# Two row tiles of the output projection inside the last group of the attention loop; the last group's sums by one product and its quotients from PSUM

## The chip, the cores and the metric

The kernel runs on one core of one Trainium2 chip. The core has a matrix engine (TensorE, PE in the profile), a vector engine (VectorE, DVE), an activation engine (ScalarE, ACT), a general engine (GpSimd, POOL) and an engine that here only issues transfers (SyncE, SP). Each works through its own instructions in order; semaphores hold an instruction back until what it needs is done. Products are written to PSUM, eight banks of 128 x 512 numbers in f32, and read from there by DVE or ACT; everything else lies in SBUF. The metric is the time of one execution on the device in microseconds (us), as the median over runs.

## The reference, cut to what matters

A two-layer encoder over 1024 tokens of width 1024. Layer 0 mixes tokens by grouped-query attention (16 query heads of width 64, 4 key/value heads), layer 1 by pooling; each layer then has a cross-attention into 256 memory tokens and a gated MLP. All of it is f32. The change lies at the end of the attention of layer 0 and at the begin of its output projection:

```python
def axial_gqa_attention(h, w_qkv, q_gain, k_gain, w_o):
    ...
        scores = jnp.einsum('bkgqd,bksd->bkgqs', q_blk, kt).astype(jnp.float32)
        p = jax.nn.softmax(scores, axis=-1).astype(vt.dtype)
        return jnp.einsum('bkgqs,bksd->bkgqd', p, vt)
    ...
    o = o.transpose(1, 0, 4, 2, 3, 5).reshape(b, s, N_HEADS * HEAD_DIM)
    return o @ w_o

x = x + axial_gqa_attention(rmsnorm(x, attn_norm[ia]), attn_w_qkv[ia],
                            attn_q_gain[ia], attn_k_gain[ia], attn_w_o[ia])
x = x + memory_cross_attention(rmsnorm(x, xattn_norm[i]), ...)
```

## The kernel before, in words

**Split products.** Every operand of an accurate product is kept as a high and a low half (`high` on ACT, `low` on DVE: the high half is the rounded number, the low half what is left). `mm3` (L758) makes one product of three matmuls: high by high (L761), high by low (L762), low by high (L763). A block of 128 rows by 512 columns of a projection over width 1024 is eight such triples, 24 matmuls, into one PSUM bank.

**The attention loop.** `attention` works through 16 groups, `G = 0..15`: a group is one half of the 1024 queries (512) and one pair of heads; groups 0 to 7 are the first half, 8 to 15 the second. A group has four steps `d = 0..3`, each with two key tiles. Per step PE makes the scores of two key tiles (`plan_scores`, L1225, into the tiles `pT`), ACT the exponentials (L1232) into a tile `X` (an `E` in the code), PE the products with the values (`plan_values`, L1267, into `pO`) one step later, and besides the scores of coming groups once more for their row maxima (`plan_peaks`, L799, into `pS`, read by DVE at L805). There are none of these left to make in the last group.

**The sums of a group.** The softmax denominators are column sums of the exponentials. DVE adds the two tiles of a step (L1276) into a scratch tile `acc[G, d]`; POOL adds these onto `acc[G, 0]` (`more`, L1279); `plan_sum` then multiplies by ones (L1303: PE, 4 matmuls for one `acc`) into a bank `pS`. In the last group, POOL adds only `acc[G, 1]`, and the product runs over three tiles, `d = 0, 2, 3`: 12 matmuls. After that comes a chain over several engines: ACT copies the sums to SBUF (L1307), a transfer brings the distinct ones to 8 x 128 (L1312), DVE takes reciprocals (L1316), two transfers (L1321, L1326) spread them out over 128 x 512 through DRAM, POOL multiplies the output by them (L1330), and ACT and POOL write high and low halves of it (L674, L1338) into the tiles `OT`, the left operand of the output projection. `OT[0]` and `OT[1]` belong to the first half of the queries, `OT[2]` and `OT[3]` to the second.

**PSUM.** In the loop there are two `pT` of two banks, three `pS` and one `pO`; a `pS` is taken by a pair of peaks (two of them) or by one sum. After the loop a pool of four `pB` of one bank and two `pA` of two lies over the same eight banks; a tile of it waits for the last reader of what was there.

**What sets the order.** The order on every engine in the loop comes from a planner (class `Plan`): `plan.add(kind, size, emit, reads, writes, take, uses, late=...)` enters an operation with a cost of its kind; PE keeps the order in which operations are entered, the others are placed by when their inputs are due to be ready and by a due time, worked back from those who read them or given by `late`. `take` names pool buffers (`("A", b)`: one of the three `pS`). Transfers are planned on SP in the same manner.

**The output projection.** Its weights come in two column halves. The first, `self.ws`, is loaded and split in group 14 (`plan_rows`: four pieces, transfer L1361, `high` and `low` at L674 and L677). The second is loaded by `load_rows` after the loop (transfer L696 into a scratch tile `scr`, L682 on ACT, L683 on DVE, four pieces). There are six scratch tiles; `acc`, `ON` (a group's output and its reciprocals) and the pieces of weights all live in them. The blocks `(n, t)`, column half `n` and row tile `t`, are made by `rows_by`: `gemm` (24 matmuls into a `pB`) and `add` (L1761, DVE adds it to `X[t]`), in the order that `Seven.begin` gives:

```python
        steps = ((0, 0), (0, 2), (1, 0), (1, 2), (0, 4), (1, 4), (0, 6), (1, 6),
                 (0, 1), (1, 1), (0, 3), (1, 3), (0, 5), (0, 7), (1, 5), (1, 7))
        turns = {3: 0, 4: 2, 6: 4, 8: 6, 10: 1, 12: 3, 15: 5}
```

After each block comes `save` (SP, L321: that half of `X[t]` to DRAM), after a second half the row's norm (ACT L742, POOL L734 and L736, DVE L325, in place on `X[t]`), and at the steps named in `turns` PE transposes a normed row tile (L330). Row tiles 0 to 3 need only `OT` of the first half of the queries; `(0, 4)` is the first that needs groups 8 to 15.

**The residual.** `plan_x` loads row tiles 0, 2, 4, 6 of `x` (L1415) into tiles that held exponentials and have come free.

Of the kernel before, what the change touches and what calls it, by code (L numbers as in the profile page):

```python
# [635 lines left out]
class Kernel:  # L636
# [140 lines left out]
    def attention(self):  # L777
# [416 lines left out]
        with tc.tile_pool(name="at", bufs=1, reuse_waits="tile") as at, self.psum("psl", 0, 0) as self.ps:  # L1194
# [63 lines left out]
            def plan_values(G, d):  # L1258
# [34 lines left out]
            def plan_sum(G):  # L1293
                half, m = GROUPS[G]
                b, own, used = ("sum", G), ("on", G, 1), [("on", G)]
                ds = (0,) if G < last else (0, 2, 3)

                def emit():
                    T[b] = self.ps.tile([P, 512], F32, name="pS", bufs=3)
                    for d in ds:  # L1300
                        u = acc.pop((G, d))
                        for x in range(2):
                            nc.tensor.matmul(T[b][x * HD:(x + 1) * HD], ones, u[:, x * 512:(x + 1) * 512],  # L1303
                                             start=d == ds[0], stop=d == ds[-1])
# [23 lines left out]

                def scale():
                    nc.gpsimd.tensor_tensor(out=ON[G][:, :512], in0=ON[G][:, :512], in1=ON[G][:, 512:], op=OP.mult)  # L1330

                def part(j, lo):
# [4 lines left out]
                    if lo:  # L1337
                        nc.gpsimd.tensor_tensor(out=l, in0=src, in1=h.bitcast(F32), op=OP.subtract)  # L1338
                    else:
                        self.high(h, src)  # L1340
                plan.add("product", 4.0 * len(ds), emit, [("acc", G, d) for d in ds], [b], [("A", b)], [("acc", G, d) for d in ds])
                plan.add("copy", 512, copy, [b, ("on", G)], [own], uses=[b, *used])
                plan.add("load", 0.2, spread, [own], [("rs", G)], uses=used)
                plan.add("recip", 128, inverse, [("rs", G)], [("rs", G)])
                plan.add("load", 0.2, park, [("rs", G)], [("inv", G)])
                plan.add("load", 0.5, back, [("inv", G)], [own], uses=used)
                plan.add("pool", 512, scale, [own, ("on", G)], [("on", G)], uses=used)
                for j in range(2):
                    k = ("OT", G, j)
                    plan.add("copy", 256, partial(part, j, 0), [("on", G)], [k], [("half", None)] * 8 if (m, j) == (0, 0) else (), used,  # L1350
                             late=14.0)
                    plan.add("pool", 256, partial(part, j, 1), [("on", G), k], [k], uses=used, late=15.0)
# [24 lines left out]

            self.ws = []
            with tc.manual_schedule():
# [5 lines left out]
                def peak():  # L1385
                    for it in [next(ahead, None)]:
                        if it:
                            plan_peaks(*it)
                for n, (G, d) in enumerate(steps):
# [359 lines left out]
    def rows_by(self, lhs, X, free, rhs, free_w):  # L1749
# [4 lines left out]
        def gemm(n, t):  # L1754
            ps[t] = self.psB()
# [3 lines left out]
        def add(n, t):  # L1759
            x = X[t][:, n * 512:(n + 1) * 512]  # L1760
# [581 lines left out]
    def run(self):  # L2342
# [14 lines left out]
        steps = self.rows_by(lhs, X, free, lambda n, k: self.blk(ws[n], k, slice(0, 512)), lambda n: R.put(*ws[n]))  # L2357
# [48 lines left out]
```

## Time and profile before

| what | value |
|---|---|
| median of 3 runs | 2414.16 us (2412.76 to 2416.49) |
| profiled execution, its own time | 2419.23 us |
| its span, first to last instruction | 2417.4 us |
| granted TensorE clock, mean | 0.997 |
| DVE busy | 78% of the span |
| ACT busy | 49% |
| POOL busy | 18% |
| the 240 reads of peaks (L805) | 152.9 us of DVE |
| the pair adds of the loop (L1276), 49 | 80.6 us of DVE |

The page of the profile gives each engine's busy time, a strip of 40 slices over the span, the chain of work that ended last, and the costliest groups of instructions. Beside it the trace answers views: the instructions of an engine in order of time (start, duration, engine, line, operation, tile written <- tiles read, count; in brackets the idle time before it and what ended that), groups by line, and busy time by stretch. A matmul's duration overlaps with that of the next; what one costs is the distance from start to start.

### The profile page before, as it was taken

What the parts mean: (1) busy time and instruction counts of PE and PEld (TensorE: products, weight loads), DVE (VectorE), ACT (ScalarE), POOL (GpSimd) and SP (SyncE); (2) the same over time, 40 slices, a digit from 0 to 9 for tenths busy, and PEclk for the clock granted to TensorE, in tenths of its full rate; (3) what the DMA queues carried; (4) which work ended last, traced back from release to release, by engine and by line L of the source; (5) the groups of instructions that cost most, each with busy time, mean ns of one, the idle gap of its engine ahead of it and who ended that gap; (6) DMA issues with size and microseconds to landing.
All of it is one profiled execution on the core that took longest, in us unless ns stands there. A gap on an engine that the chain in (4) does not pass through costs nothing.

```text
span 2417.4 us, 33999 instructions
## 1 busy us (share of the span) xinstructions
PE 2392.6 (99%) x12484; PEld 1939.3 (80%) x12484; DVE 1887.3 (78%) x2689; ACT 1182.0 (49%) x1894; POOL 426.1 (18%) x465
## 2 busy tenths in 40 slices
PE   8999999999999999999999999999999999999998
PEld 8984544688998888888888888798888888887887
DVE  6789999549873798888887767987389888888875
ACT  6335556425562555455454427555255554545442
POOL 6757777410010000000000003011000000000001
PEclk9999999999999999999999999999999999999999
DMA  7000001425951234333387533696123332338852
GB/s 254 19 2 10 19 15 45 139 89 191 322 199 44 88 98 129 109 88 109 103 288 243 190 100 124 205 324 216 51 86 113 105 109 87 114 119 272 261 187 101
DMA packets 323004, 324.41 MB, mean 134 GB/s; under 512 B 32533, under 2 KB 253053, under 8 KB 322837
## 3 DMA queue, kind: packets, MB, share of 16 engines
q1 hardware_dynamic: 322837, 322.23, 41.5%
q8 instruction: 99, 1.62, 0.3%
q14 instruction: 68, 0.56, 0.1%
HBM read 234.58 MB, written 82.64 MB: 131 GB/s over the span
## 4 chain that ended last, share of the span: by engine, by line
PE 90%; DVE 3%; issue 3%; DMA 2%; POOL 1%; ACT 1%; SPq 0%; POOLq 0%; DVEq 0%; ACTq 0%
PE pB L761 23%; PE pB L763 23%; PE pB L762 22%; PE pO L1267 4%; PE pT L1225 3%; PE pA L763 3%; PE pA L761 3%; PE pA L762 3%; PE pS L799 2%; DVE R L677 1%; PE pB L330 1%; PE pS L1303 1%; PE pA L2282 0%; DMA scr<-X 0%; DMA scr<-in_ffn_w_down 0%
## 5 line engine op out<-in xcount | busy, mean ns | idle before, releaser
L761 PE MATMUL pB<-R,R 128*128 128x512 f32 (+1 forms) x2764 | 1026.0, 371 | 3.7 <-DVE scr L446 1.2
L763 PE MATMUL pB<-R,R 128*128 128x512 f32 (+1 forms) x2760 | 1018.3, 369 | 1.4 <-DVE R L677 1.2
L762 PE MATMUL pB<-R,R 128*128 128x512 f32 (+1 forms) x2764 | 1019.3, 369 | 0.2 <-DVE R L677 0.2
L761 PEld LDWEIGHTS pB<-R,R 128*128 128x128 f32 x2764 | 522.6, 189 | 95.4 <-DVE scr L446 2.5
L763 PEld LDWEIGHTS pB<-R,R 128*128 128x128 f32 x2760 | 521.8, 189 | 89.5 <-DVE R L677 3.2
L762 PEld LDWEIGHTS pB<-R,R 128*128 128x128 f32 x2764 | 522.8, 189 | 86.3 <-DVE R L677 1.2
L674 ACT ACTIVATE R<-scr 128x512 fp32r<-128x512 f32 (+3 forms) x372 | 268.7, 750 | 230.6 <-DMA scr<-Gs 59.3
L734 POOL TENSOR_SCALAR ms<-ss 128x1 f32<-128x1 f32 (+2 forms) x93 | 26.0, 280 | 1655.6 <-ACT R L742 1284.1
L677 DVE TENSOR_TENSOR R<-X,R 128x512 fp32r<-128x512 f32 x374 | 253.1, 689 | 67.8 <-ACT R L674 67.2
L677 DVE TENSOR_TENSOR R<-scr,R 128x512 fp32r<-128x512 f32 (+2 forms) x332 | 283.8, 884 | 25.7 <-ACT R L674 25.1
L674 ACT ACTIVATE R<-X 128x512 fp32r<-128x512 f32 x374 | 231.9, 630 | 133.4 <-PE pB L762 64.0
L444 ACT COPY scr<-pB 128x512 f32<-128x512 f32 x156 | 91.1, 584 | 180.1 <-PE pB L763 172.9
L805 DVE TENSOR_REDUCE nm<-pS 128x1 f32<-128x512 f32 x240 | 152.9, 684 | 18.2 <-PE pS L799 16.4
L1970 DVE TENSOR_TENSOR X<-pB,X 128x512 f32<-128x512 f32 (+1 forms) x145 | 99.4, 687 | 82.3 <-PE pB L763 81.2
L1232 ACT ACTIVATE X<-pT 128x1024 f32<-128x1024 f32 x128 | 125.2, 1023 | 76.6 <-PE pT L1225 73.0
L761 PE MATMUL pA<-R,R 128*128 128x512 f32 (+1 forms) x420 | 150.6, 358 | 0.0
L763 PE MATMUL pA<-R,R 128*128 128x512 f32 (+1 forms) x420 | 150.2, 358 | 0.0
L762 PE MATMUL pA<-R,R 128*128 128x512 f32 (+1 forms) x420 | 150.0, 357 | 0.0
L1267 PE MATMUL pO<-X,X 128*64 128x512 f32 x512 | 123.8, 605 | 0.0
L446 DVE TENSOR_TENSOR scr<-pB,scr 128x512 f32<-128x512 f32 x156 | 107.2, 687 | 11.5 <-PE pB L763 11.4
L1225 PE MATMUL pT<-R,R 64*128 64x512 f32 x768 | 104.7, 393 | 1.3 <-ACT X L1232 1.3
L1815 DVE SCALAR_TENSOR_TENSOR scr<-scr,conv 128x1023 f32<-128x1023 f32 x66 | 84.7, 1284 | 20.9 <-ACT scr L1810 18.9
(179 smaller groups left out, 2882.3 us busy)
## 6 DMA issues: line engine op xcount, KB each, us to landing
X<-in_ffn_w_up SPq DMA_DIRECT2D x82, 512.0 KB
Gs<-X SPq DMA_DIRECT2D x105, 256.0 KB
scr<-in_ffn_w_down SPq DMA_DIRECT2D x45, 512.0 KB
scr<-Gs SPq DMA_DIRECT2D x35, 512.0 KB
scr<-in_xattn_w_kv SPq DMA_DIRECT2D x32, 512.0 KB
scr<-Gs SPq DMA_DIRECT2D x42, 384.0 KB
Wt<-scr SPq DMA_DIRECT2D x44, 256.0 KB
Gs<-scr SPq DMA_DIRECT2D x42, 256.0 KB
```

The source lines that it names most:

```text
L444: self.nc.scalar.copy(out, p)
L446: self.nc.vector.tensor_tensor(out=out, in0=p, in1=out, op=OP.add)
L674: self.nc.scalar.activation(hi, src, AF.Copy)
L677: self.nc.vector.tensor_tensor(out=lo, in0=src, in1=hi.bitcast(F32), op=OP.subtract)
L761: mm(out, ah, bh, start=start, stop=False)
L762: mm(out, ah, bl, start=False, stop=False)
L763: mm(out, al, bh, start=False, stop=stop)
L805: nc.vector.tensor_reduce(NM[G][:, 2 * n + x.start:2 * n + x.stop], S, axis=AX.X, op=OP.max, negate=True)
L1225: nc.tensor.matmul(T[G, kt % 2][:, x * 512:(x + 1) * 512], left, right, start=first and (i, j) == (0, 0), stop=shifted or (not first and i ...
L1232: nc.scalar.activation(E[G, kt], T[G, kt % 2], AF.Exp)
L1267: nc.tensor.matmul(O[G][x * HD:(x + 1) * HD], V32[kt // 4][:, kt % 4, m // 4 * 2 + x], E[G, kt][:, x * 512:(x + 1) * 512], start=kt == 0, ...
L1970: nc.vector.tensor_tensor(out=x, in0=banks[b][:, c], in1=x, op=OP.add)
```

## The change

1. **Blocks (0, 0) and (0, 2) move into the loop.** A new `plan_out(t, ks)` enters products of a block for the `k` in `ks`, into a tile `pS`; `plan_added(t)` enters the add. In the last group, where a place for peaks finds none left, one triple of block (0, 0) is entered: eight places, eight triples. Block (0, 2) is entered whole, between the last products with the values and the last sum. The two adds are entered after the last sum; nothing in the plan reads what they write. `rows_by` skips both blocks' `gemm` and `add`; the saves stay.
2. **The last group's sums by one product.** `acc[15, 2]` and `acc[15, 3]` are added onto `acc[15, 0]` by DVE (`acc[15, 1]` still by POOL), and 4 matmuls replace 12.
3. **The last group's quotients from PSUM.** In place of copy, transfer, small reciprocal and two transfers, DVE takes the reciprocal of the 128 x 512 sums straight out of the bank `pS` (`direct`); scaling and low halves of this group go from POOL to DVE.
4. **Group 14's halves later.** Its `high` and `low` are entered after the loads of `x`, and the `high` waits for the last exponentials.

```diff
-                def more(other):
-                    nc.gpsimd.tensor_tensor(out=acc[G, 0], in0=acc[G, 0], in1=other(), op=OP.add)
+                def more(other, engine=nc.gpsimd):
+                    engine.tensor_tensor(out=acc[G, 0], in0=acc[G, 0], in1=other(), op=OP.add)
...
+                elif d and mine:
+                    plan.add("add", 1024, partial(more, lambda: acc.pop((G, d)), nc.vector), [u, ("acc", G, d)], [u],
+                             uses=[u, ("acc", G, d)], late=5.0)
...
-                ds = (0,) if G < last else (0, 2, 3)
...
-                    for d in ds:
-                        u = acc.pop((G, d))
-                        for x in range(2):
-                            nc.tensor.matmul(T[b][x * HD:(x + 1) * HD], ones, u[:, x * 512:(x + 1) * 512],
-                                             start=d == ds[0], stop=d == ds[-1])
+                    u = acc.pop((G, 0))
+                    for x in range(2):
+                        nc.tensor.matmul(T[b][x * HD:(x + 1) * HD], ones, u[:, x * 512:(x + 1) * 512], start=True, stop=True)
...
+                def direct():
+                    nc.vector.reciprocal(ON[G][:, 512:], T.pop(b))
+
+                engine, kind = (nc.gpsimd, "pool") if G < last else (nc.vector, "add")
...
+                plan.add("product", 4.0, emit, [("acc", G, 0)], [b], [("A", b)], [("acc", G, 0)])
+                if G < last:
...
+                else:
+                    plan.add("recip", 720, direct, [b, ("on", G)], [own], uses=[b, *used])
+                plan.add(kind, 512, scale, [own, ("on", G)], [("on", G)], uses=used)
+
+                def parts(*after):
+                    for j in range(2):
+                        k = ("OT", G, j)
+                        plan.add("copy", 256, partial(part, j, 0), [("on", G), *after], [k],
+                                 [("half", None)] * 8 if (m, j) == (0, 0) else (), used, late=14.0)
+                        plan.add(kind, 256, partial(part, j, 1), [("on", G), k], [k], uses=used, late=15.0)
+                if G == last - 1:
+                    return parts
+                parts()
...
+            def plan_out(t, ks):
+                b = ("out", t)
+
+                def emit():
+                    if not ks[0]:
+                        T[b] = self.ps.tile([P, 512], F32, name="pS", bufs=3)
+                    for k in ks:
+                        ah, al = (R.v(s, 8)[:, k, t // 2 * P:(t // 2 + 1) * P] for s in OT[0])
+                        self.mm3(T[b], ah, al, *self.blk(self.ws, k, slice(0, 512)), k == 0, k == NK - 1, True)
+
+                plan.add("product", 3 * len(ks), emit, [(("ws", k // 4, k % 4 // 2), 0) for k in ks] + [("OT", G, 0) for G in range(NH // 2)],
+                         [b], () if ks[0] else [("A", b)])
+
+            def plan_added(t):
+                b = ("out", t)
+
+                def add():
+                    x = X[t][:, :512]
+                    nc.vector.tensor_tensor(out=x, in0=T.pop(b), in1=x, op=OP.add)
+                plan.add("add", 512, add, [b, ("X", t)], [("X", t)], uses=[b])
...
+                    it = next(ahead, None)
+                    if it:
+                        plan_peaks(*it)
+                    elif G == last:
+                        plan_out(0, [next(fill)])
+                fill = iter(range(NK))
...
-                        plan_sum(G - 1)
+                        parts = plan_sum(G - 1)
...
                 for t in (0, 2):
                     plan_x(t)
+                parts(("E", last, NT - 1))
                 plan_values(last, 3)
+                plan_out(2, range(NK))
                 plan_sum(last)
+                for t in (0, 2):
+                    plan_added(t)
...
-    def rows_by(self, lhs, X, free, rhs, free_w):
+    def rows_by(self, lhs, X, free, rhs, free_w, done=()):
...
+            if (n, t) in done:
+                return
...
-        steps = self.rows_by(lhs, X, free, lambda n, k: self.blk(ws[n], k, slice(0, 512)), lambda n: R.put(*ws[n]))
+        steps = self.rows_by(lhs, X, free, lambda n, k: self.blk(ws[n], k, slice(0, 512)), lambda n: R.put(*ws[n]), ((0, 0), (0, 2)))
```

More of the change, by code (lines that the diff above doesn't have):

```diff
@@ L1337, in part @@
                     if lo:
-                        nc.gpsimd.tensor_tensor(out=l, in0=src, in1=h.bitcast(F32), op=OP.subtract)
+                        engine.tensor_tensor(out=l, in0=src, in1=h.bitcast(F32), op=OP.subtract)
                     else:
                         self.high(h, src)
-                plan.add("product", 4.0 * len(ds), emit, [("acc", G, d) for d in ds], [b], [("A", b)], [("acc", G, d) for d in ds])
-                plan.add("copy", 512, copy, [b, ("on", G)], [own], uses=[b, *used])
@@ L1343, in plan_sum @@
[L1343 to L1352, printed above, removed]
+                plan.add("product", 4.0, emit, [("acc", G, 0)], [b], [("A", b)], [("acc", G, 0)])
```

12 lines of the change are left out of this document (8 added, 4 removed).

## The prediction

> **What bounds the kernel now.** I read the page first, then busy time by stretch around the end of the loop, then PE, ACT, POOL and DVE in order of time there.
>
> ```profile
> span 2417.4 us, 33999 instructions
> PE 2392.6 (99%) x12484; PEld 1939.3 (80%) x12484; DVE 1887.3 (78%) x2689; ACT 1182.0 (49%) x1894; POOL 426.1 (18%) x465
> ```
>
> PE is busy for 2392.6 of 2417.4 us. So work that only changes its place on PE moves nothing; the time changes by PE work that goes away, by PE idle time that goes away, and by new idle time. The stretches below are the last group up to its third step, its rest with the last sum, the blocks (0, 0) and (0, 2), and block (1, 0) up to block (0, 4); the columns are start:end, length, then busy time (instructions) of PE, PEld, DVE, ACT, POOL, then clock, DMA share, GB/s.
>
> ```profile
> 427.55:438.28 10.73, 10.73 (x67) 5.12 (x67) 8.92 (x4) 6.91 (x8) 10.49 (x5) 1.00 0.21 74
> 438.28:449.34 11.06, 9.04 (x47) 3.03 (x43) 6.45 (x5) 5.23 (x8) 6.67 (x4) 1.00 0.61 197
> 449.34:460.39 11.05, 11.05 (x48) 9.12 (x49) 5.23 (x6) 4.75 (x6) 3.81 (x3) 1.00 0.82 277
> 460.39:472.06 11.67, 11.67 (x57) 9.74 (x56) 4.19 (x5) 1.88 (x4) 3.48 (x5) 1.00 0.20 71
> ```
>
> All idle time is in the second stretch: 11.06 - 9.04 = 2.02 us. PE in order of time names its two pieces:
>
> ```profile
> 438.28 1.03 PE L1303 MATMUL pS<-scr,ones 128*64 128x512 f32 x4
> 439.23 0.96 PE L1225 MATMUL pT<-R,R 64*128 64x512 f32 x6
> 441.53 0.96 PE L1225 MATMUL pT<-R,R 64*128 64x512 f32 x6 [1.33 <-ACT X L1232]
> 442.42 3.65 PE L1267 MATMUL pO<-X,X 128*64 128x512 f32 x16
> 445.91 2.74 PE L1303 MATMUL pS<-scr,ones 128*64 128x512 f32 x12
> 449.34 0.50 PE L761 MATMUL pB<-R,R 128*128 128x512 f32 x1 [0.69 <-ACT scr L1307]
> 449.68 0.40 PE L762 MATMUL pB<-R,R 128*128 128x512 f32 x1
> 449.92 0.40 PE L763 MATMUL pB<-R,R 128*128 128x512 f32 x1
> ...
> 460.39 0.39 PE L761 MATMUL pB<-R,R 128*128 128x512 f32 x1
> ```
>
> The first, 1.33, is the last scores waiting for an exponential. ACT and POOL say why it was late: group 13's high half (L674) stood ahead of it on ACT and waited for POOL's scaling.
>
> ```profile
> 439.84 0.72 ACT L674 ACTIVATE R<-scr 128x256 fp32r<-128x256 f32 x2 [2.83 <-POOL scr L1330]
> 448.70 0.58 ACT L1307 COPY scr<-pS 128x512 f32<-128x512 f32 x1 [1.95 <-PE pS L1303]
> ...
> 437.55 2.27 POOL L1330 TENSOR_TENSOR scr<-scr 128x512 f32<-128x512 f32 x1
> ```
>
> The second, 0.69, is the one to look at. The first block after the loop starts 0.06 after ACT has copied the last sum (448.70 + 0.58 = 449.28): the first `pB` lies on the bank of the last sum, and waits for that bank's reader. This is the wait that the change touches.
>
> **Part by part.** *Moved blocks.* The 48 matmuls of (0, 0) and (0, 2) took 11.05 us where they stood, and take them again: nothing by itself. They do push the loop's other engines apart: seven triples of 0.7 us come before the stalled scores, about 5 us, and ACT had cleared its wait by 440.56. So the 1.33 goes (to 0 at best; it stays whole if ACT slips by as much). Next late behind it is nothing on PE: the last exponentials have the 3.65 us of L1267 to run under.
>
> Each triple stands between products of another shape, and that costs an entry:
>
> ```profile
> 416.18 1.55 PE L1225 MATMUL pT<-R,R 64*128 64x512 f32 x12
> 417.57 0.43 PE L799 MATMUL pS<-R,R 64*128 64x512 f32 x2
> ...
> 419.79 1.66 PE L1225 MATMUL pT<-R,R 64*128 64x512 f32 x12
> 421.38 1.94 PE L1267 MATMUL pO<-X,X 128*64 128x512 f32 x8
> ```
>
> Twelve scores behind their like take 1.39 (416.18 to 417.57), behind L1267 1.59 (419.79 to 421.38): 0.2 an entry. Into a triple it is 0.34 - 0.24 = 0.1 (449.34, 449.68, 449.92). Eight triples add an entry each, 0.8 to 1.6 with the lower bound at 0; I take 0.9.
>
> *One product for the sums.* From the chain of waits, 4 matmuls against 12, and three rows of DVE in order of time:
>
> ```profile
> 406.75 0.86 PE pS L1303 x4
> ...
> 446.08 2.60 PE pS L1303 x12
> ...
> 431.94 3.40 DVE L1276 TENSOR_TENSOR scr<-X,X 128x1024 f32<-128x1024 f32 x1
> 435.45 3.22 DVE L677 TENSOR_TENSOR R<-scr,R 128x1024 fp32r<-128x1024 f32 x1
> ...
> 445.28 1.28 DVE L1276 TENSOR_TENSOR scr<-X,X 128x1024 f32<-128x1024 f32 x1
> ```
>
> That removes 1.74 us of PE work. In its place DVE adds two tiles of 128 x 1024 behind the last pair add. Such an add takes 1.28 when POOL rests and up to 3.40 beside POOL, so 2.6 to 6.8, under the 3.65 us of L1267 and the 5.5 of block (0, 2): nothing on the path. Uncovered it would be 2.6.
>
> The triples' weights: the fourth piece's low half ended at 435.45 + 3.22 = 438.67 and is wanted by the seventh triple at about 444. That hides it; without these 5 us PE would wait.
>
> *Quotients from PSUM.* A reciprocal of 128 x 512 isn't in the trace. Two smaller ones are:
>
> ```profile
> L1316 DVE RECIPROCAL rs<-rs 8x128 f32<-8x128 f32 x16 | 14.9, 932 | 4.2 <-DMA rs<-scr 4.2
> L1581 DVE RECIPROCAL inv<-sum 128x4 f32<-128x4 f32 x16 | 2.8, 174 | 8.7 <-ACT X L1576 8.7
> ```
>
> (932 - 174) / 124 = 6.1 ns an element of a row, so 174 + 508 x 6.1 = 3.28 us; the upper bound is four times the 128-element one, 3.73. The Trainium skill, "VectorE: DVE Perf Modes", "First, the fixed hardware budget", has the reciprocal as an iterated divide with a repeat count of 8; at that page's 0.96 GHz I estimate 4.3 us and a sum 1.0 higher, and these rows, at 5.9 cycles an element, don't bear it out.
>
> Now where it lies. During the end of the loop two of the three `pS` are kept by (0, 0) and (0, 2) until their adds, which come last on DVE as nothing in the plan waits for them. The last sum can only get the third, group 14's, freed by a copy. The three go round in turn, and one tile more, that of (0, 0), ahead of group 14's sum puts that sum where the last one lay before: again the buffer under the first `pB`. So block (1, 0), now first after the loop, waits for the reciprocal: 3.28 and two hand-overs of 0.05, 3.4 in place of 0.69. The gap was filled by a 0.58 copy and will be filled by a long DVE instruction. Bounds: 0, should the bank be another, and 3.8.
>
> What else left: five transfer issues of group 15 on SP, ACT's copy, POOL's scaling and low halves. None was on the path; OT of group 15 is wanted by block (0, 4), 11.67 us after (1, 0) starts.
>
> *DVE's queue.* DVE is in order, and the reciprocal shares it with the second column half's low halves:
>
> ```profile
> 453.12 1.23 DVE L683 TENSOR_TENSOR R<-scr,R 128x1024 fp32r<-128x1024 f32 x1 [6.56 <-ACT R L682]
> 454.26 0.93 DVE L1316 RECIPROCAL rs<-rs 8x128 f32<-8x128 f32 x1
> 457.23 1.31 DVE L683 TENSOR_TENSOR R<-scr,R 128x1024 fp32r<-128x1024 f32 x1 [2.04 <-ACT R L682]
> ...
> 459.06 2.35 DVE L683 TENSOR_TENSOR R<-scr,R 128x1024 fp32r<-128x1024 f32 x2
> ```
>
> The last sum will end at 448.65 + 11.05 - 1.74 - 1.33 + 0.9 = 457.5. The second low half ran from 457.23 here; ahead of the reciprocal it costs 1.3, behind it the third and fourth come at 462 and 463.5, when block (1, 0) wants them at 463.6 and 465. Between 0 and 2.6 (two of them ahead); I take 0.4.
>
> *The clock.* One gap of this size is in the trace:
>
> ```profile
> 29.71 0.69 PE L1062 MATMUL pB<-ident,kr 128*128 128x128 f32 x2 [3.59 <-POOL kr L1038]
> ...
> 25.53:28.94 3.41, 0.59 (x6) 0.39 (x4) 2.34 (x8) 2.54 (x6) 2.20 (x5) 1.00 0.90 300
> 28.94:35.77 6.83, 6.06 (x29) 6.06 (x30) 6.41 (x13) 4.50 (x9) 5.81 (x9) 0.50 0.42 146
> ...
> 438.54:441.95 3.41, 2.08 (x14) 0.86 (x12) 2.74 (x3) 2.11 (x5) 2.88 (x3) 1.00 0.86 302
> ```
>
> After 3.59 us without PE the granted clock was 0.50 for 6.83 us; after a stretch of 3.41 with 2.08 busy it stayed 1.00. A gap of 3.8 is like the first. Dense matmuls at half clock lose half of the time: 0 to 3.4; I take one half of the stretch, 1.7, as part of it can lie under the gap. The Trainium skill, "TensorE: Matmul & The Clock Gate", "Part 1: The HAM clock gate (the "warmup" mystery)", lets the clock fall after at least one idle window of about 3.4 us, free-running; by that a gap of 3.8 would hold a whole window in one case of nine, and the sum would be without the 1.7. The trace differs: that clock fell with 0.59 of the 3.41 us before it busy.
>
> **The sum**, against the profiled execution's own 2419.23 us (its span and 1.83 around it): -1.74 (sums) - 1.33 (stall) + 0.9 (entries) + 2.7 (3.4 for 0.69) + 0.4 (queue) + 1.7 (clock) = +2.6, so 2421.8. That execution was 5.07 above the median of the runs; with the same distance the median becomes 2416.8.
>
> **The rivals.**
>
> *No fall of the clock.* The gap is there, and two stretches share it so that neither is idle enough: +0.9, 2415.1. For it speaks 438.54 to 441.95, against it 25.53 to 28.94. The Trainium skill's page named above would expect this one.
>
> *No new wait.* The first `pB` lies on a bank that is free early: -1.74 - 1.33 - 0.69 + 0.9 = -2.9, 2411.3; with entries at nothing -3.8, 2410.4. Against it: the 0.06 between copy and product here.
>
> *Slower: the reciprocal queues on DVE behind weights.* A low half of (n = 1) whose transfer waits for a scratch tile that the last additions free stands ahead of it. How long such a piece takes:
>
> ```profile
> 455.62 0.37 SPq L696 DMA_DIRECT2D scr<-in_attn_w_o  x1
> ...
> 459.02 1.06 ACT L682 ACTIVATE R<-scr 128x1024 fp32r<-128x1024 f32 x1 [0.87 <-DMA scr<-in_attn_w_o]
> ```
>
> 3.4 to landing, 1.06, 1.25: with a tile freed about 453, the third low half ends at 459.7, 2.2 behind the sum; the gap becomes 6, the clock loses its 3.4: 0.5 + 2.2 + 3.4 = +6.1, 2420.3. Were it the fourth piece, whose tile the last sum itself frees, it would be 5.7 in place of 2.2: 2423.8. It decides if the reciprocal starts over 1.5 us behind the last sum's end. Row 454.26 shows that order once, row 457.23 the other.
>
> *The triples don't fill.* One waits for its weights or the last exponentials stay late; the 1.33 stays: +3.9, 2418.1.
>
> **How the numbers follow.** Forecast 0.48 (own range 2414.5 to 2419), no fall of the clock 0.19, no new wait 0.15, DVE's queue 0.12, triples 0.06. 80 in 100 lie in 2410.5 to 2421: from the lower end of no new wait to just past the third-piece case. A measurement here tells 0.2%, 4.8 us, from no change. Under 2409.3 no case reaches; I leave 0.06 for what I don't see. Over 2419.0 lie the queue, 0.12, and the forecast with two stretches at half clock and dear entries, 0.11: 0.23. Within: 0.71.
>
> **What would show it.** Right: block (1, 0) preceded by 3.4 to 4 us of idle time ended by DVE's reciprocal, no wait in the last scores, L1303 with 64 matmuls, and a stretch at clock 0.50 from about 459 to 463. Wrong: a first product after the loop with under 1 us before it; a reciprocal far from 3.3 us; triples with waits ahead of them; or PE idle later, where block (0, 4) waits for group 15.

## The result and the profile after

The changed kernel takes 2420.29 us (median of 15 runs, 2418.01 to 2425.08), the one before on the same chip 2414.12 us (15 runs, 2411.61 to 2418.83): a ratio of 1.0023, interval 1.0016 to 1.0030, so 3.9 to 7.2 us more. Forecast was 2416.8, range 2410.5 to 2421.0.

The spans say less than this, and in the other direction: the profiled execution of the changed kernel, the fastest of its 15, took 2418.01 us against 2419.23.

```profile
span 2416.2 us, 33972 instructions
```

The execution of before had the half clock for 6.83 us from 28.94, shown ahead of the prediction, and for 3.41 us from 1489.84, both far from the change; in the changed kernel's it came at neither place. So the two are compared over one stretch: from PE's first instruction of the last group to the first transposes (L330), which follow block (1, 2). Before, PE in order of time gives the end of that stretch as

```profile
471.27 1.03 PE L330 MATMUL pB<-ident,X 128*128 128x128 f32 x8
```

and its start as 427.55 (the six scores shown ahead of the prediction): 43.72 us. PE in order of time for the changed kernel, with the two last scores' neighbours, the end of the loop and the first block behind it:

```profile
424.06 0.50 PE L761 MATMUL pS<-R,R 128*128 128x512 f32 x1
...
427.00 0.50 PE L761 MATMUL pS<-R,R 128*128 128x512 f32 x1
...
427.90 1.94 PE L1267 MATMUL pO<-X,X 128*64 128x512 f32 x8
...
442.02 1.65 PE L1225 MATMUL pT<-R,R 64*128 64x512 f32 x12
...
444.50 3.65 PE L1267 MATMUL pO<-X,X 128*64 128x512 f32 x16
448.08 0.50 PE L761 MATMUL pS<-R,R 128*128 128x512 f32 x1
...
453.79 1.08 PE L1304 MATMUL pS<-scr,ones 128*64 128x512 f32 x4
458.42 0.47 PE L761 MATMUL pB<-R,R 128*128 128x512 f32 x1 [3.55 <-DVE scr L1330]
459.40 0.50 PE L762 MATMUL pB<-R,R 128*128 128x512 f32 x1 [0.51 <-DVE R L683]
...
463.62 0.40 PE L761 MATMUL pB<-R,R 128*128 128x512 f32 x1
464.13 0.50 PE L762 MATMUL pB<-R,R 128*128 128x512 f32 x1
...
472.20 1.03 PE L330 MATMUL pB<-ident,X 128*128 128x128 f32 x8
```

472.20 - 424.06 = 48.14: the stretch is 4.4 us longer, inside the interval of the runs. The reader is to see four things. The twelve scores at 442.02 have no bracket: the stall of 1.33 is gone. A triple among products of another shape takes 0.90 (427.00 to 427.90), where a dense one takes 0.68. Block (1, 0) starts after an idle time of 3.55 that DVE's reciprocal ended, and its second matmul waits once more, for a low half of the weights (L683). And the fifth triple's second matmul, 464.13, comes 0.51 behind the first, where dense matmuls are 0.23 apart. What it waits for stands in DVE's order of time:

```profile
454.91 3.36 DVE L1330 RECIPROCAL scr<-pS 128x512 f32<-128x512 f32 x1 [7.33 <-PE pS L1304]
458.19 1.16 DVE L683 TENSOR_TENSOR R<-scr,R 128x1024 fp32r<-128x1024 f32 x1
459.26 0.68 DVE L1335 TENSOR_TENSOR scr<-scr 128x512 f32<-128x512 f32 x1
459.86 1.22 DVE L683 TENSOR_TENSOR R<-scr,R 128x1024 fp32r<-128x1024 f32 x1
461.00 0.76 DVE L1343 TENSOR_TENSOR R<-scr,R 128x256 fp32r<-128x256 f32 x2
461.67 1.28 DVE L1409 TENSOR_TENSOR X<-pS,X 128x512 f32<-128x512 f32 x2
462.87 2.35 DVE L683 TENSOR_TENSOR R<-scr,R 128x1024 fp32r<-128x1024 f32 x2
```

No row behind the first has a bracket: DVE works without a pause from 454.91, and the third low half, the first of the two at 462.87, ends near 464.1. From the end of the last sum (454.87) to there PE has had 13 matmuls to do, 3.0 us of work at 0.23 each. Busy time by stretch shows the clock (columns as ahead of the prediction):

```profile
453.02:456.44 3.42, 1.84 (x8) 0.57 (x6) 1.53 (x1) 2.55 (x4) 2.25 (x3) 1.00 0.75 283
456.44:459.85 3.41, 0.92 (x3) 0.59 (x4) 3.41 (x3) 1.86 (x3) 0.00 (x0) 1.00 0.82 303
459.85:463.27 3.42, 3.42 (x10) 2.65 (x9) 3.42 (x7) 0.87 (x3) 0.00 (x0) 0.50 0.02 9
```

The clock was 0.50 for one stretch. Its matmuls stand 0.43 apart, but at full clock PE would only have come sooner to the third low half, and waited for it until 464.1 (e3 below bears on that). So three things lie over one another here: the bank under the reciprocal, DVE's queue, and the clock.

### The profile page after: what moved, and what is told of

It is laid out like the page before. It is cut to its first block, busy times and chain, and to the rows that moved or that the text cites. A ratio compares the mean times of both kernels' runs of the same rounds, so it can differ in the third digit from the quotient of the medians.

```text
span 2416.2 us, 33972 instructions
## 1 busy us (share of the span) xinstructions
PE 2391.3 (99%) x12476; PEld 1935.6 (80%) x12476; DVE 1893.0 (78%) x2694; ACT 1181.1 (49%) x1893; POOL 424.2 (18%) x462
## 4 chain that ended last, share of the span: by engine, by line
PE 92%; issue 3%; DVE 3%; POOL 1%; DMA 1%; ACT 1%; SPq 0%; POOLq 0%; DVEq 0%; ACTq 0%
PE pB L761 23%; PE pB L763 22%; PE pB L762 22%; PE pO L1267 5%; PE pT L1225 4%; PE pA L763 3%; PE pA L761 3%; PE pA L762 3%; PE pS L799 2%; PE pB L330 1%; DVE R L677 1%; PE pS L1304 1%; PE pA L2327 0%; DMA scr<-X 0%; DMA Xq<-X 0%
```

## The experiments

The stretch of each, from its own PE rows as above, stands in the table at the end of this section; each is that of one execution. A stretch of half clock costs some 1.7 us (below), so differences smaller than that between two stretches are not read without the medians. The ratios are against the kernel before on the same chip, whose medians there were 2414.8 to 2415.3 us. Line numbers in e1, e10 and e12 shift by one, and in e8 the product is L1306.

**e1_bank**: the last sum in another bank.

```diff
-                    T[b] = self.ps.tile([P, 512], F32, name="pS", bufs=3)
+                    T[b] = (self.ps.tile([P, 1024], F32, name="pT", bufs=2)[:, :512] if G == last
+                            else self.ps.tile([P, 512], F32, name="pS", bufs=3))
...
-                plan.add("product", 4.0, emit, [("acc", G, 0)], [b], [("A", b)], [("acc", G, 0)])
+                plan.add("product", 4.0, emit, [("acc", G, 0)], [b], [("B" if G == last else "A", b)], [("acc", G, 0)])
```

> The changed kernel, with its last sum written to a pT tile (banks 3 to 6) and not to the pS under the first pB; nothing else. The stretch meant below runs from PE's first instruction of the last group to the first transposes (L330): 43.7 us before (427.55 to 471.27), 48.1 changed (424.06 to 472.20). Theory 1, the bank: the loss is the 3.55 us that block (1, 0) waits for the reciprocal to leave its bank, and the stretch at half clock behind it. Then block (1, 0) starts within 0.3 us of the last sum's end, no clock of 0.50 follows, the stretch is 43 us and the time about 1 us below the kernel before. Rival, DVE's queue: the first low half of the second column half (L683) stands behind the reciprocal on DVE (458.19 after 454.91 to 458.27) and would hold the second matmul of block (1, 0) just as long. Then L761 starts early, but L762 waits some 3.5 us for L683, the clock falls as before, the stretch stays at 47.5 to 48.5 and the time 4 to 6 us above the kernel before. Second rival, entries of the triples: the loss is not in the gap; no change either, but also without a new wait at L762.

Measured: 2420.55 us, ratio 1.0025 (1.0015 to 1.0034). PE and DVE in order of time:

```profile
456.63 0.50 PE L761 MATMUL pB<-R,R 128*128 128x512 f32 x1 [1.38 <-ACT R L682]
459.79 0.80 PE L762 MATMUL pB<-R,R 128*128 128x512 f32 x1 [2.66 <-DVE R L683]
...
455.30 3.36 DVE L1331 RECIPROCAL scr<-pT 128x512 f32<-128x512 f32 x1 [7.35 <-PE pT L1305]
458.58 1.16 DVE L683 TENSOR_TENSOR R<-scr,R 128x1024 fp32r<-128x1024 f32 x1
```

The wait for the bank is gone, and nothing is gained: the first rival, DVE's queue, came about. The first matmul now waits for a high half of the weights, the second for its low half, which stands behind the reciprocal in DVE's order. The clock fell as well, for 6.83 us.

**e2_sum_first**: the last sum ahead of block (0, 2).

```diff
-                plan_out(2, range(NK))
                 plan_sum(last)
+                plan_out(2, range(NK))
```

> The changed kernel with the last sum entered ahead of block (0, 2) and not behind it, so that the reciprocal of 3.36 us can run under the 5.5 us of that block. Theory 1, the bank: the gap at block (1, 0) falls below 0.7 us, no clock of 0.50, stretch 43 us, time 1 us below the kernel before. Rival, DVE's queue and what feeds it: block (1, 0) then waits for the first low half of its weights (L683), which waits for ACT's L682 behind group 14's L674; ACT was held by that until 453.9 in the changed kernel, so that low half comes about 456.8, 1.5 to 2.5 us after the end of block (0, 2); clock 1.00 or 0.50 by chance; stretch 45 to 46, time 1 to 2.5 us above the kernel before. Entries of the triples: stretch as changed, 48.

Measured: 2417.40 us, ratio 1.0009 (1.0000 to 1.0018). PE in order of time:

```profile
458.86 0.47 PE L761 MATMUL pB<-R,R 128*128 128x512 f32 x1 [1.67 <-DVE X L1409]
```

The reciprocal ran from 451.55 under block (0, 2). Block (1, 0) still waited, 1.67 for the add of a moved block (L1409), as its first `pB` now lies on an output's bank, and 0.73 for a low half (462.91). There was no fall of the clock here. With the reciprocal under cover 3.7 of the 4.4 us go.

**e3_filled**: 14 matmuls into a free `pT` in the gap; their result is not used.

```diff
...
+                    for _ in range(14):
+                        nc.tensor.matmul(p[:, :512], ah, self.blk(self.ws, 0, slice(0, 512))[0], start=True, stop=True)
+                plan.add("product", 14, fill_gap, (), ["fill"], [("B", "fill")])
```

> The changed kernel with 14 more matmuls of 128x128 by 512 behind the last sum, into a pT tile that nobody reads: 3.2 us of PE work inside the gap of 3.55. It adds work and removes no wait. If the half clock comes from the idle gap: no clock of 0.50 there, the stretch is 1.6 shorter, 46.5 us, and the time 1.5 us below the changed kernel. If the fall of the clock is independent of the gap: the clock of 0.50 stays in some place within 5 us, stretch 48.1, no change of the time. If the gap is not where the time is lost, entries of the triples: no change either.

Measured: 2422.02 us, ratio 1.0032 (1.0020 to 1.0043). PE in order of time, then by stretch:

```profile
456.38 3.47 PE L1450 MATMUL pT<-R,R 128*128 128x512 f32 x14
460.00 0.47 PE L761 MATMUL pB<-R,R 128*128 128x512 f32 x1
460.99 0.50 PE L762 MATMUL pB<-R,R 128*128 128x512 f32 x1 [0.51 <-DVE R L683]
...
466.49 0.54 PE L762 MATMUL pB<-R,R 128*128 128x512 f32 x1 [2.12 <-DVE R L683]
```

```profile
463.39:466.81 3.42, 1.30 (x6) 0.77 (x5) 3.42 (x6) 0.23 (x1) 0.00 (x0) 1.00 0.37 146
466.81:470.22 3.41, 3.41 (x9) 2.64 (x8) 0.76 (x1) 0.00 (x0) 0.00 (x0) 0.50 0.02 8
```

The clock held over the filled gap. But at full clock PE came sooner to the third low half, waited 2.12 for it, and then the clock fell. Taking the half clock out of the gap uncovered DVE's queue. As a price of the clock alone the run is inconclusive, since the queue was also longer here: the fourth piece's transfer came later, its high half on ACT (461.95) held up the attention's high halves, and DVE waited 0.68 for those ahead of the third low half.

**e4_whole**: no triples in the loop; block (0, 0) whole ahead of (0, 2).

```diff
-                    elif G == last:
-                        plan_out(0, [next(fill)])
...
+                plan_out(0, range(NK))
                 plan_out(2, range(NK))
```

> The changed kernel without triples: block (0, 0) is entered whole, ahead of block (0, 2), and nothing fills the places between the scores. Entries of the triples: eight entries go, measured at 1.5 us together, and the last scores' stall of 1.33 comes back. Theory 1, the bank, and DVE's queue alike: the gap and the half clock at block (1, 0) stay, stretch 48 (48.1 - 1.5 + 1.3), time as the changed kernel within 1 us. If the triples are the loss: stretch 45 or less and the time within 1 us of the kernel before.

Measured: 2426.39 us, ratio 1.0048 (1.0035 to 1.0060). PE and DVE in order of time:

```profile
465.19 0.77 PE L761 MATMUL pB<-R,R 128*128 128x512 f32 x1 [9.58 <-DVE X L1409]
...
455.64 3.56 DVE L683 TENSOR_TENSOR R<-scr,R 128x1024 fp32r<-128x1024 f32 x3 [2.89 <-ACT R L682]
459.12 3.35 DVE L1330 RECIPROCAL scr<-pS 128x512 f32<-128x512 f32 x1
...
464.36 1.28 DVE L1409 TENSOR_TENSOR X<-pS,X 128x512 f32<-128x512 f32 x2
```

The clock was 0.50 for 10.24 us from 457.77, most of it under the wait. Here the order on DVE that the third rival of the prediction described came about: low halves ahead of the reciprocal. Without the triples the first `pB` lies on a bank whose reader is the add, last of all on DVE, and 1.27 of the stall in the last scores is back. So the triples do take that stall away, and they turn the buffers so that the bank is only the reciprocal's.

**e5_short_queue**: the last group's scaling and low halves on POOL again, the moved blocks' adds due at once.

```diff
-                engine, kind = (nc.gpsimd, "pool") if G < last else (nc.vector, "add")
+                engine, kind = nc.gpsimd, "pool"
...
-                plan.add("add", 512, add, [b, ("X", t)], [("X", t)], uses=[b])
+                plan.add("add", 512, add, [b, ("X", t)], [("X", t)], uses=[b], late=0.0)
```

> The changed kernel with DVE's queue shortened behind the reciprocal: the last group's scaling and low halves go back to POOL, and the adds of blocks (0, 0) and (0, 2) get an early due time, so they run ahead of the reciprocal. The bank, the reciprocal and the gap stay. Stretch as before: 43.7 us before, 48.1 changed. Theory 3, weights through DVE's queue: in the changed kernel the third low half (L683, ends 464.1) stood behind scaling, low halves and adds, and the rest of the stretch follows it by 8.1 us, so the half clock ran under that wait. Now the third low half ends about 461.9 and is in time; what is left is the gap of 3.5, 0.5 for the first low half, and the half clock, now uncovered: stretch 47.5 to 48 with a clock of 0.50, 46.3 without; no wait at the fifth k of block (1, 0). Theory 1, the bank and the clock as the whole loss: stretch 48.1, nothing changes. Time 3 to 5 us above the kernel before in both; the waits inside block (1, 0) tell them apart.

Measured: 2420.96 us, ratio 1.0024 (1.0014 to 1.0033). PE waits 3.55 and 0.52, as long as in the changed kernel (the trace puts the first down to ACT's high halves, L682, the third of which ended 0.14 us behind the reciprocal; the two can't be told apart here). The clock falls for 3.41, and there is no wait behind it; the four low halves follow the reciprocal directly. A shorter queue alone gains nothing clear (0.4 us of the stretch; the ratio is that of the changed kernel), because the half clock, until then under the queue, now sets the pace.

**e6_old_quotients**: the third part undone (copy, transfers and small reciprocal of before; POOL as in e5).

```diff
-                if G < last:
+                if G <= last:
                     plan.add("copy", 512, copy, [b, ("on", G)], [own], uses=[b, *used])
```

> The changed kernel with the third part undone: the last group's sums are copied by ACT and its quotients go the old way (transfer, small reciprocal, two transfers, POOL). Blocks, triples and the one product stay. Neither the bank nor DVE is held by a long reciprocal. Theory 1, the bank: gap 0.7, no clock of 0.50, stretch 43, time 1 us below the kernel before. Theory 3, weights: block (1, 0) starts after 0.7 but waits for the first low half some 1 to 2 us (ACT's L682 behind group 14's L674) and about 0.5 for the fourth (its transfer starts when the last sum frees a scratch tile); stretch 44.3 to 45, clock 1.00, time 0.3 to 1.5 us above the kernel before.

Measured: 2418.68 us, ratio 1.0018 (1.0009 to 1.0026); the stretch, 47.21, is above both expectations. PE's rows with idle time:

```profile
456.24 0.50 PE L761 MATMUL pB<-R,R 128*128 128x512 f32 x1 [1.33 <-ACT scr L1307]
...
457.09 0.49 PE L762 MATMUL pB<-R,R 128*128 128x512 f32 x1 [0.35 <-DVE R L683]
...
462.71 0.50 PE L762 MATMUL pB<-R,R 128*128 128x512 f32 x1 [1.25 <-DVE R L683]
...
471.33 1.09 PE L330 MATMUL pB<-ident,X 128*128 128x128 f32 x8 [1.75 <-DVE X L325]
```

Without the long reciprocal the clock holds, and the waits go to four places: the copy stands behind other work on ACT, two low halves are late, and the first transposes wait for a norm whose square (L742) stood behind group 15's high halves on ACT. So the reciprocal alone is not the cause either.

**e7_one_block**: as e6, and block (0, 2) stays behind the loop.

```diff
-                plan_out(2, range(NK))
...
-                for t in (0, 2):
-                    plan_added(t)
+                plan_added(0)
...
```

> As e6_old_quotients, but block (0, 2) stays behind the loop, where the kernel before had it; only the eight triples of (0, 0) move. Theory 3, weights: block (0, 2) is again the cover under which the second column half arrives, and the scratch tiles come free 5.5 us earlier; no wait over 0.5 in block (1, 0), stretch 42.2 (43.7 - 1.74 for the sums - 1.33 for the stall + 1.5 for the entries), time 1.5 us below the kernel before. If the triples themselves are the loss: stretch 45 or more and the time above the kernel before.

Measured: 2418.38 us, ratio 1.0013 (1.0004 to 1.0022); a miss by 5 us of the stretch. The rival's bound (45 or more) is met in number, but not by the triples: up to the last sum the stretch is 5.55 us longer than before, with 5.48 us of moved products in it. The loss lies behind it. Block (1, 0) waited 0.59, 1.42, 0.81, 0.47 and 1.49, the second time for a high half of the weights, else for low halves. ACT in order of time:

```profile
456.98 0.72 ACT L674 ACTIVATE R<-scr 128x256 fp32r<-128x256 f32 x2 [2.44 <-POOL scr L1335]
457.61 1.04 ACT L682 ACTIVATE R<-scr 128x1024 fp32r<-128x1024 f32 x1
459.76 1.06 ACT L682 ACTIVATE R<-scr 128x1024 fp32r<-128x1024 f32 x1 [1.11 <-DMA scr<-in_attn_w_o]
462.21 1.06 ACT L682 ACTIVATE R<-scr 128x1024 fp32r<-128x1024 f32 x1 [1.39 <-DMA scr<-in_attn_w_o]
```

The first piece (453.48), the third and the fourth wait for their transfer, the second stands behind the attention's high halves, which wait for POOL. What (0, 0) and (0, 2) did behind the loop was to cover this loading, with 11 us of work. With one block moved, half of the cover is gone.

**e8_sums_only**: the kernel before with the second part alone.

```diff
...
+                elif d and mine:
+                    plan.add("add", 1024, partial(more, lambda: acc.pop((G, d)), nc.vector), [u, ("acc", G, d)], [u],
+                             uses=[u, ("acc", G, d)], late=5.0)
...
-                ds = (0,) if G < last else (0, 2, 3)
+                ds = (0,)
```

> The kernel before with the second part of the change alone: DVE adds acc 2 and 3 of the last group onto acc 0, and one product of 4 matmuls replaces 12. If the one product is a gain by itself: stretch 43.7 - 1.74 = 42.0, time 1.7 us below the kernel before. Rival, the cover: without block (0, 2) ahead of the sum the two additions lie open; DVE has its last pair add at 445.3 to 446.5 and needs one or two more of 1.23 behind it, and POOL's own addition ends at 445.5, so the sum starts about 448.2 in place of 445.9: stretch 43.7 - 1.74 + 2.3 = 44.3, time 0.5 us above the kernel before or the same.

Measured: 2420.29 us, ratio 1.0022 (1.0012 to 1.0032). PE in order of time:

```profile
447.60 1.98 PE L1306 MATMUL pS<-scr,ones 128*64 128x512 f32 x4 [3.90 <-DVE scr L1279]
```

The rival came about, and dearer than its 44.3: the four matmuls wait 3.90 us for DVE's additions, which have nothing over them, and the clock falls for 6.83. In the changed kernel block (0, 2) covers the additions: its last sum has no wait.

**e9_no_weights**: the second column half's weights neither loaded nor split.

```diff
-        ws.append(self.load_rows(a["attn_w_o"][0], 1))
+        ws.append([R.get() for _ in range(4)])
...
-lambda n, k: self.blk(ws[n], k, slice(0, 512)), lambda n: R.put(*ws[n])
+lambda n, k: self.blk(ws[0], k, slice(0, 512)), lambda n: R.put(*ws[1 - n])
```

> The changed kernel without the load and the split of the second column half's weights: the blocks (1, t) take the first half's (so their results are not the reference's); the slots are still taken and given back. Up to the first transposes of the row tiles the stretch was 43.7 us before, 48.1 changed. Theory 3 (the wait for the bank under the reciprocal, the split weights behind it on DVE, and the half clock lie over one another, so that taking one away uncovers the next): the gap of 3.55 ahead of block (1, 0) stays, as DVE's reciprocal alone gives it, the 0.51 behind it goes, the clock still falls for 3.41: 46.5 to 47.6. Rival (the weights alone make the loss, the bank is free by the time they come): no gap over 1 us, no fall, 42 to 43.

Measured: 2420.14 us, ratio 1.0020 (1.0012 to 1.0029); stretch 47.76, just over the 47.6 of the first theory, as the clock fell for 6.83 instead of 3.41. PE in order of time, and the stretch ahead of the fall:

```profile
458.37 0.80 PE L761 MATMUL pB<-R,R 128*128 128x512 f32 x1 [3.46 <-DVE scr L1330]
```

```profile
453.50:456.91 3.41, 1.41 (x6) 0.20 (x4) 1.95 (x1) 0.72 (x2) 1.66 (x3) 1.00 0.00 0
```

With the weights out of the way the bank still holds PE, and the clock does the rest.

**e10_neither**: the edits of e1 and e9 together.

> The same without the weights, and the last sum in a tile pT, another bank, as in e1_bank (which had 49.0). Theory 3: both causes are gone, so no gap over 0.3 us ahead of block (1, 0) and no fall of the clock; left are the sums -1.74, the idle time of before -2.02 and the triples' entries +1.5, which gives 41.4; 41.2 to 42.4, and a time 0.9988 to 1.0002 of the kernel's before. Rival (a third cause that the runs so far have not named, in the triples or on ACT): 44 or more with PE idle or slow at another place.

Measured: 2414.37 us, ratio 0.9996 (0.9987 to 1.0005), stretch 41.75, as theory 3 has it. PE in order of time, and DVE's reciprocal beside it:

```profile
455.31 1.08 PE L1305 MATMUL pT<-scr,ones 128*64 128x512 f32 x4
456.32 0.50 PE L761 MATMUL pB<-R,R 128*128 128x512 f32 x1
...
456.44 3.36 DVE L1331 RECIPROCAL scr<-pT 128x512 f32<-128x512 f32 x1 [7.36 <-PE pT L1305]
```

No idle time, no fall of the clock. One cause away gains nothing clear (e1 48.95, e9 47.76 against 48.14; ratios 1.0025 and 1.0020 against 1.0023), both away gain 6.4. Either one is enough to hold PE and bring the clock down; that is what "lie over one another" means in numbers.

**e11_sum_first_short**: e2 and e5 together, with the real weights.

> Real weights: the last sum ahead of block (0, 2) as in e2_sum_first (44.4), the two additions of the moved blocks due at once, and the last group's scaling and low halves on POOL again as in e5_short_queue. Theory 3: the reciprocal runs under block (0, 2), DVE's queue behind it holds low halves alone, and block (1, 0) waits only for the addition of (0, 2), 0.7 us, in place of 1.67 and 0.73: 42.5 to 43.3, a time 0.9993 to 1.0011 of the kernel's before. Rival (the weights' transfers are late by themselves, whatever DVE does): a wait of 1.5 us or more ended by ACT's L682 or by DMA, 44 or more.

Measured: 2422.82 us, ratio 1.0030 (1.0018 to 1.0043); stretch 49.63: a miss, and the rival's wait came. Block (1, 0) waited 0.88 for the add as expected, then 0.24, 2.64 and 0.64, and the clock fell for 6.83 us. ACT in order of time:

```profile
460.57 0.72 ACT L674 ACTIVATE R<-scr 128x256 fp32r<-128x256 f32 x2 [2.44 <-POOL scr L1335]
461.80 0.72 ACT L674 ACTIVATE R<-scr 128x256 fp32r<-128x256 f32 x2 [0.51 <-POOL scr L1335]
462.43 1.99 ACT L682 ACTIVATE R<-scr 128x1024 fp32r<-128x1024 f32 x2
```

Of the two explanations it was neither DVE's queue behind the reciprocal nor the weights' transfer: the third piece's high half stood on ACT behind two groups' high halves, which waited for POOL. POOL in turn could start only at 458.37, since DVE had made group 14's small reciprocal only at 449.41 (in the changed kernel at 444.30), and now it had two groups to scale. Giving POOL the scaling back emptied DVE's queue and made ACT's.

**e12_before_mended**: the kernel before, with high halves entered later and the last sum in a `pT`.

```diff
+                if G == last - 1:
+                    return parts
+                parts()
...
+                parts(("E", last, NT - 1))
                 plan_values(last, 3)
...
-                    T[b] = self.ps.tile([P, 512], F32, name="pS", bufs=3)
+                    T[b] = (self.ps.tile([P, 1024], F32, name="pT", bufs=2)[:, :512] if G == last
+                            else self.ps.tile([P, 512], F32, name="pS", bufs=3))
```

> The kernel before with two small edits and none of the change's blocks: group 13's high halves are entered behind the last exponentials (this takes the 1.33 away), and the last sum lies in a tile pT, so that the first pB after the loop does not wait for its copy (0.69). Theory: 43.7 - 1.33 - 0.69 = 41.7, 41.4 to 42.3, a time 0.9987 to 0.9999 of the kernel's before. Rival (the freed time is taken by the next wait: weights of the second half, OT of group 15 or the bank of another tile): 43 or more, with a new wait in the blocks.

Measured: 2414.02 us, ratio 0.9995 (0.9986 to 1.0004); stretch 43.43. The first edit missed its aim: `last - 1` is group 14, and the halves in the way are group 13's. They still stand ahead of the last exponentials (group 14's sum is only made at 435.80), and the stall is 1.83. PE, then ACT in order of time:

```profile
435.80 1.03 PE L1304 MATMUL pS<-scr,ones 128*64 128x512 f32 x4
...
439.55 0.96 PE L1225 MATMUL pT<-R,R 64*128 64x512 f32 x6 [1.83 <-ACT X L1232]
...
437.86 0.72 ACT L674 ACTIVATE R<-scr 128x256 fp32r<-128x256 f32 x2 [3.33 <-POOL scr L1331]
438.49 1.00 ACT L1232 ACTIVATE X<-pT 128x1024 f32<-128x1024 f32 x1
```

The 0.69 behind the last sum is gone, and most of it came back as a longer stall. The time can't be told from before; a version of this with group 13's halves moved was not tried.

| kernel | PE's first of the last group | first transposes | stretch |
|---|---|---|---|
| before | 427.55 | 471.27 | 43.72 |
| changed | 424.06 | 472.20 | 48.14 |
| e1_bank | 424.46 | 473.41 | 48.95 |
| e2_sum_first | 426.56 | 470.99 | 44.43 |
| e3_filled | 425.65 | 476.16 | 50.51 |
| e4_whole | 425.01 | 477.49 | 52.48 |
| e5_short_queue | 424.85 | 472.57 | 47.72 |
| e6_old_quotients | 424.12 | 471.33 | 47.21 |
| e7_one_block | 424.42 | 472.02 | 47.60 |
| e8_sums_only | 425.48 | 473.49 | 48.01 |
| e9_no_weights | 424.12 | 471.88 | 47.76 |
| e10_neither | 425.60 | 467.35 | 41.75 |
| e11_sum_first_short | 425.88 | 475.51 | 49.63 |
| e12_before_mended | 425.07 | 468.50 | 43.43 |

## Why the prediction was right, and where it was short

The likeliest case came about: the sums, the stall, the gap under the reciprocal and the fall of the clock, each where it was expected. One link, DVE's queue, was worked out wrongly. The size was +2.6 us, the stretch shows +4.4 and the medians +6.2, and the measured median lies only 0.7 us inside the upper end of the range. Term by term, from the rows shown:

- *Sums, -1.74.* The four matmuls took 1.08 (453.79), the twelve 2.74 (445.91 to 448.65): -1.66. e8 shows what the cover was worth: without it the part costs 4.3 us of the stretch, not the 2.6 - 1.74 that the prediction's price without cover would leave, since the wait of 3.90 brought the clock down.
- *Stall, -1.33.* Gone; e4, without the triples, has 1.27 of it back.
- *Entries, +0.9.* Too small. The last products with the values start 20.44 behind the stretch's first instruction (444.50 - 424.06), before 14.87 (442.42 - 427.55): 5.57 more. Eight dense triples are 24 x 0.2285 = 5.48 (before, 96 matmuls from 449.34 to 471.27 took 21.93), less the stall of 1.33; so the entries are 1.42. Block (0, 2) took 5.71 to the last sum (448.08 to 453.79) for 5.48 dense, another 0.2. Together 1.6: the upper bound of the prediction.
- *The gap, 3.4 for 0.69.* 3.55, ended by the reciprocal of 3.36 (estimated 3.28 from two smaller ones). The buffers went round as worked out. The estimate from the Trainium skill's "VectorE: DVE Perf Modes", 4.3 us, does not agree with 3.36.
- *DVE's queue, +0.4.* This is the step that fell short. The prediction had the third and fourth low halves behind the reciprocal "at 462 and 463.5, when block (1, 0) wants them at 463.6 and 465". It counted the reciprocal and low halves of the weights in that queue, and left out what the change itself moved there: scaling (0.68), group 15's low halves (0.76) and the two adds (1.28), 2.7 us in all ahead of the third one, which ended at 464.1. It also worked out when PE wants them at full clock, 2.7 us behind the block's start, while it put 1.7 us of half clock into the sum beside the queue. With the half clock PE came to the fifth triple 5.2 us behind the start (458.42 to 463.62) and still had to wait. So queue and clock lie over one another and were added as if they did not.
- *Half clock, +1.7.* One stretch of 3.42, from 459.85. Seven of its matmuls span 2.98 (460.07 to 463.05) where dense ones take 1.6, and its edges add 0.3: 1.7. That the size fits is luck: the prediction halved the price of the 6.83 us seen at 28.94, as a part could lie under the gap; what came was a stretch of half that length, all of it behind the gap.

With the new terms the sum is -1.66 - 1.33 + 1.6 + 2.9 (gap) + 1.2 (the 0.51, 0.25 more ahead of that second matmul, and 0.4 at the fifth triple) + 1.7 = +4.4; the queue and the entries make nearly all of the difference to +2.6. But as prices the last three can't be added or taken away singly, and that the prediction did not say. In the stretch e5 took the queue and got 0.4 back, e3 filled the gap and lost 2.4, e1 took the bank and lost 0.8; by their ratios none of the three differs clearly from the changed kernel. e2, which put the reciprocal under a block, got 3.7 back, and e10, without bank and weights, 6.4.

Of the rivals, the fall of the clock was rightly preferred to no fall; "no new wait" was wrong; the queue behind the weights came about not in the changed kernel but in e4; the triples filled. The price of that queue rival has a slip: 453 + 3.4 + 1.06 + 1.25 is 458.7 and not 459.7, which makes the case 2419.3 and not 2420.3. The range's upper end was set just past it, and the measured 2420.29 lies just there, so that the range holds it is in part luck. The remaining 1.8 us between stretch and medians lies inside the interval and wasn't followed.

## What to carry to other kernels

Work that is moved off a place takes its cover with it: list what was loaded, split or copied under it, and when the next block wants that. Where several waits end close together, add up each engine's in-order string (here DVE's 9.2 us from the last sum to the third low half) and take the longest, rather than a sum of waits; an experiment that removes one of them may show nothing (e1, e5, e9) until the others are removed too. A short product in place of a long one was a gain here only with another block over the additions that it needs (e8).

## What the runs showed of the hardware

In these traces the clock changed on a raster of 3.41 us. Around the change it fell to 0.50 after stretches of 3.41 us with 0.92 (changed kernel), 1.30 (e3) and 1.41 us (e9) of PE work in them (less in e1, e4, e5, e8 and e11), and not after one with 1.84 (453.02 to 456.44, changed kernel) or 1.74 (456.28 to 459.69, e2). In e3 the longest idle time in that stretch was 2.12 us, so a wait of 2 us can cost the clock if it falls into one stretch; it takes less than the 3.59 us that the trace of before showed. Busy time alone does not decide it everywhere: before, at 1489.84, the clock also fell after a stretch with 3.25 us of PE work counted in it, much of it products of 24 x 16 numbers. The Trainium skill's "TensorE: Matmul & The Clock Gate", Part 1, lets the clock fall after at least one idle window of about 3.4 us. These traces differ: every one of the stretches named here had PE work in it.

Around the change the half clock ended after the first stretch that PE filled nearly or wholly: one stretch in the changed kernel (3.42 busy), two in e9 (1.95, then 3.42) and e11 (2.67, then 3.42), three in e4 (0, 0, then 2.82). A wait that still goes on at half clock makes it last longer.

A triple of 128 x 128 by 512 put between matmuls of another shape took 0.90 us, in a row 0.68; eight of them put singly cost 1.4 us more than the same 24 matmuls in a row.
